# Rotating 96 images by 90 degrees: hand-placed semaphores and loads cut into 32 KB reads

## The chip, the cores and the metric

The kernel runs on one core of a Trainium2 chip. A core has several engines that run side by side; here three matter. VectorE (DVE in the profile) transposes blocks. SyncE (SP) and ScalarE (ACT) only issue transfers: SP issues the loads from DRAM into the core's on-chip memory, ACT issues the stores back to DRAM. The transfers themselves are carried out by 16 DMA engines, which both queues share. The on-chip memory has 128 partitions; a tile is written `[partitions, elements]`.

The metric is the device time of one execution in microseconds (us), the median of several runs.

## The reference

```python
def setup_inputs():
    batch, c, h, w = 32, 3, 256, 256
    return {"x": np.random.randn(batch, c, h, w).astype(np.float32)}

def reference(x):
    return np.rot90(x, k=1, axes=(-2, -1)).astype(np.float32)
```

Each of the 96 images of 256 x 256 float32 values (256 KB) is turned by 90 degrees: `out[i, j] = x[j, 255 - i]`. No arithmetic is done; 25.17 MB are read and 25.17 MB written.

## The kernel before

The 96 images are worked in six groups of G = 16 images (4.19 MB). A group is loaded into a tile S, turned from S into a tile U, and U is stored. There are three buffers for S and three for U. A tile framework sets the semaphores: it makes SP wait before it loads into an S buffer that is still being read, makes VectorE wait for loads and for U buffers still being stored, and makes ACT wait for the transposes. Within an engine, instructions run in program order.

VectorE's `transpose` works on blocks of 32 partitions by 32 elements. Partitions hold neighbouring rows of an image, so a block transposition moves data between the 32 partitions of a group of 32, and the access patterns of source and destination, with `::-1` where the order is reversed, do the rest of the rotation within a partition. No transfer needs to reach elements one by one: each partition is filled from one contiguous run in DRAM and emptied into one.

Two kinds of groups are used (`KINDS = [1, 2, 2, 2, 2, 1]`):

- Kind 1, the first and the last group: the group is cut into four parts of 1 MB. A partition holds R = 8 rows of an image, a run of 8 KB. Four loads (L44) are issued, then for each part one transpose of 128 x 2048 elements (L49) and one store (L50).
- Kind 2, the four groups between: a partition holds R = 16 rows, runs of 16 KB. Two loads of 2 MB each (L60) fill the two halves of S. Then 16 transposes of 128 x 512 elements (L65) read both halves, and two stores of 2 MB each (L67) empty U.

All loads stand in SP's queue and all stores in ACT's. In the trace the loads' DMA queue is q1 and the stores' is q10. The DMA engines see a transfer as packets, one for each contiguous run (8 KB or 16 KB here), plus small ones (under 512 B) that announce completion, 16 for each transfer.

Of the kernel before, what the change touches and what calls it, by code (L numbers as in the profile page):

```python
# [1 line left out]

# [4 lines left out]


@with_exitstack
def kernel(  # L10
    ctx: ExitStack,
    tc: tile.TileContext,
    x: bass.AP,
    out: bass.AP,
):
    nc = tc.nc
    B, C, H, W = x.shape
    assert H == W == 256
    N = B * C
    P = 128  # L20
    G = 16
    KINDS = [1, 2, 2, 2, 2, 1]
    assert len(KINDS) * G == N
    F = G * H * W // P
    fp32 = mybir.dt.float32

    xf = x.rearrange("b c h w -> (b c h w)").rearrange("(g f) -> g f", g=N // G)
    of = out.rearrange("b c h w -> (b c h w)").rearrange("(g f) -> g f", g=N // G)

    in_pool = ctx.enter_context(tc.tile_pool(name="in_pool", bufs=3))  # L30
    out_pool = ctx.enter_context(tc.tile_pool(name="out_pool", bufs=3))

    for g, kind in enumerate(KINDS):
        S = in_pool.tile([P, F], fp32, name="S")
        U = out_pool.tile([P, F], fp32, name="U")
        if kind == 1:

            R = 8
            Sv = S.rearrange("p (s f) -> p s f", s=4)
            Uv = U.rearrange("p (s f) -> p s f", s=4)  # L40
            xv = xf[g].rearrange("(s p f) -> s p f", s=4, p=P)
            ov = of[g].rearrange("(s p f) -> s p f", s=4, p=P)
            for s in range(4):
                nc.sync.dma_start(out=Sv[:, s], in_=xv[s])  # L44
            for s in range(4):

                src = Sv[:, s].rearrange("p (r k q) -> p q r k", r=R, q=R)[:, ::-1, :, ::-1]
                dst = Uv[:, s].rearrange("p (q k r) -> p q r k", q=R, r=R)
                nc.vector.transpose(dst, src)  # L49
                nc.scalar.dma_start(out=ov[s], in_=Uv[:, s])  # L50
        else:


            R = 16
            Sv = S.rearrange("p (b f) -> p b f", b=2)
            Uv = U.rearrange("p (a f) -> p a f", a=2)
            xv = xf[g].rearrange("(b a qk f) -> b qk a f", b=2, a=2, f=F // 2)
            ov = of[g].rearrange("(b a qk f) -> a qk b f", b=2, a=2, f=F // 2)
            for b in range(2):
                nc.sync.dma_start(out=Sv[:, b], in_=xv[b])  # L60

            src = Sv.rearrange("p b (r k q) -> p q r k b", r=R, q=R)[:, ::-1, :, ::-1]
            dst = Uv.rearrange("p a (q k r) -> p q r k a", q=R, r=R)
            for q in range(R):
                nc.vector.transpose(dst[:, q], src[:, q])  # L65
            for a in range(2):
                nc.scalar.dma_start(out=ov[a], in_=Uv[:, a])  # L67


# [1 line left out]
_INS = ['x']  # L71
_OUTS = [((32, 3, 256, 256), 'float32')]


# [23 lines left out]
```

## Time and profile before

| What | Value |
|---|---|
| Median of 3 runs | 123.97 us (123.87 to 124.13) |
| The profiled execution | 124.01 us |
| Its span, first to last instruction | 122.2 us |
| VectorE busy | 91.3 us (75%), 72 transposes |
| DMA moved | 50.34 MB, 412 GB/s over the span |
| First load issued by SP | 0.73 us |
| First transpose starts | 5.67 us |
| First store issued by ACT | 9.67 us |
| Last transpose | from 106.87 us, 3.97 us long |
| Transfers issued | 16 loads and 16 stores |

Times are counted from the start of the span. Busy time of VectorE is the time in which an instruction runs on it; neighbouring transposes overlap a little, so the sum of single durations is somewhat above it. A DMA share of 1.00 means that all 16 DMA engines had packets under way for the whole window (slightly more than 1.00 can show, since packets at a window's edge are counted to it with their bytes). The list of DMA issues gives the time from issue to landing: a median of 21.1 us for a 2 MB load and 19.0 us for a 2 MB store, 16.6 and 16.1 us for those of 1 MB. That is long beside what 2 MB take at 412 GB/s (5.1 us): the transfers queue behind each other.

### The profile page before, as it was taken

How to read it: one execution, taken by the hardware profiler on the slowest of the kernel's cores; microseconds unless marked ns; L12 is line 12 of the kernel's file. 1: busy time of each engine (PE TensorE's matmuls, PEld its weight loads, DVE VectorE, ACT ScalarE, POOL GpSimd, SP SyncE). 2: the span in 40 equal slices, each digit the busy share in tenths (PEclk: the TensorE clock that was granted, in tenths of full speed). 3: DMA queues.
4: the chain of work that ended last, by engine and by line, in shares of the span. 5: the costliest groups of instructions: out<-in, count | busy, mean ns of one | idle time of the engine just before them, and what ended most of it. 6: DMA issues, size and time to landing. Idle time of an engine off the chain costs nothing.

```text
span 122.2 us, 170 instructions
## 1 busy us (share of the span) xinstructions
DVE 91.3 (75%) x72; POOL 0.2 (0%) x4
## 2 busy tenths in 40 slices
DVE  0199999007999999999999990799999999092000
POOL 0000000000000000000000000000000000000000
DMA  3999999999999999999999999999999999999993
GB/s 86 424 421 416 375 432 429 426 410 442 418 440 437 437 434 418 429 434 429 429 429 429 434 429 421 453 410 413 464 413 429 445 416 426 442 429 408 429 429 161
DMA packets 4609, 50.34 MB, mean 412 GB/s; under 512 B 512, under 2 KB 512, under 8 KB 512
## 3 DMA queue, kind: packets, MB, share of 16 engines
q1 hardware_dynamic: 2304, 25.17, 49.3%
q10 hardware_dynamic: 2304, 25.17, 48.3%
q14 instruction: 1, 0.01, 0.0%
HBM read 25.17 MB, written 25.17 MB: 412 GB/s over the span
## 4 chain that ended last, share of the span: by engine, by line
DMA 61%; DVE 27%; issue 1%; SPq 1%
DMA S<-in_x_dram 46%; DVE U L65 24%; DMA out_dram<-U 16%; DVE U L49 3%; SPq L44 1%
## 5 line engine op out<-in xcount | busy, mean ns | idle before, releaser
L65 DVE STREAM_TRANSPOSE U<-S 128x512 f32<-128x512 f32 x64 | 60.5, 1059 | 10.8 <-DMA S<-in_x_dram 7.1
L49 DVE STREAM_TRANSPOSE U<-S 128x2048 f32<-128x2048 f32 x8 | 31.0, 3937 | 8.7 <-DMA S<-in_x_dram 8.7
L82 POOL MEMSET const-bfloat16-1.0<- 128x1 bf16 x1 | 0.1, 101 | 0.0
L82 POOL MEMSET const-uint8-127<- 128x1 uint8 x1 | 0.1, 101 | 0.0
L82 POOL MEMSET const-float32-0.0<- 128x1 f32 x1 | 0.1, 98 | 0.2 <-issue 0.2
L82 POOL MEMSET const-float32-1.0<- 128x1 f32 x1 | 0.1, 98 | 0.0
## 6 DMA issues: line engine op xcount, KB each, us to landing
S<-in_x_dram SPq DMA_DIRECT2D x8, 2048.0 KB, 21.1
out_dram<-U ACTq DMA_DIRECT2D x8, 2048.0 KB, 19.0
S<-in_x_dram SPq DMA_DIRECT2D x8, 1024.0 KB, 16.6
out_dram<-U ACTq DMA_DIRECT2D x8, 1024.0 KB, 16.1
```

The source lines that it names most:

```text
L44: nc.sync.dma_start(out=Sv[:, s], in_=xv[s])
L49: nc.vector.transpose(dst, src)
L65: nc.vector.transpose(dst[:, q], src[:, q])
L82: nc = _bacc.Bacc("TRN2", target_bir_lowering=False, num_devices=1)
```

## The change

The kernel leaves the tile framework's pools and is synchronised by hand. Everything is inside one critical section (`tc.tile_critical()`), with tensors and semaphores of its own.

- A group is now G = 8 images (2.10 MB), so there are NG = 12 groups, all of one kind. There are six buffers S and six buffers U, 16 KB a partition each.
- A group is loaded in M = 2 halves of 1 MB. A partition gets RI = 8 rows, 8 KB, from each half.
- The loads of group 0 are as those of kind 1 before: 128 runs of 8 KB (L72 of the new kernel). All others go through `load`, which writes out the DMA instruction itself, so that its two sides keep their own shapes: the DRAM side is 32 rows of 8192 elements (32 KB each), the on-chip side 128 partitions of 2048 elements (8 KB each). One 32 KB read fills four partitions.
- Eight transposes of 128 x 512 elements turn a group. Those of one group differ in the row r; each reads, for every column offset q and counting back over k, the two halves b, and writes with a step of eight elements.
- A group is stored with one transfer of 2.10 MB in runs of 16 KB.
- Semaphores: `loaded[s]` counts the landing of a buffer's two loads, `turned` the groups transposed, `stored[u]` the landing of a store. SP waits for `turned` before it loads into a buffer again (group 6 on); VectorE waits for `loaded`, and from group 6 on for `stored`; ACT waits for `turned`. SP closes by waiting for all six `stored`.

The order of instructions on each engine that comes out: SP has 24 loads, the first twelve with no wait; VectorE has 96 transposes, of which the first of each group waits; ACT has 12 stores, each with one wait. SP begins with a NoOp and a branch on which SP, ACT and VectorE wait, and ends with the six waits, another NoOp and a branch that all engines follow.

```diff
-    G = 16
-    KINDS = [1, 2, 2, 2, 2, 1]
+    M = 2
+    G = 4 * M
+    RI, RO = 8, 8 * M
+    FI, FO = RI * W, RO * W
+    FOLD = 32
+    NG = N // G
+    NS = NU = 12 // M
...
+    xv = xf.rearrange("(g b d f) -> g b d f", g=NG, b=M, d=FOLD)
+    xp = xf.rearrange("(g b p f) -> g b p f", g=NG, b=M, p=P)
+    ov = of.rearrange("(g b qk f) -> g qk b f", g=NG, b=M, f=FO)
...
+    def load(dst, src):
+        return nc.sync.add_instruction(
+            mybir.InstDMACopy(
+                name=nc.get_next_instruction_name(),
+                engine=mybir.EngineType.SP,
+                ins=[fixed(src)],
+                outs=[fixed(dst)],
+                queue="qSPDynamicHW",
+                mode="Copy",
+            )
+        )
...
+    ctx.enter_context(tc.tile_critical())
+    S = [ctx.enter_context(nc.sbuf_tensor(f"S{i}", [P, M, FI], fp32)) for i in range(NS)]
+    U = [ctx.enter_context(nc.sbuf_tensor(f"U{i}", [P, FO], fp32)) for i in range(NU)]
...
+    for g in range(NG):
+        s, u = g % NS, g % NU
+        if g >= NS:
+            nc.sync.wait_ge(turned, g - NS + 1)
+        for b in range(M):
+            if g == 0:
+                d = nc.sync.dma_start(out=S[s][:, b], in_=xp[g, b])
+            else:
+                d = load(S[s][:, b], xv[g, b])
+            d.then_inc(loaded[s], 16)
+
+        nc.vector.wait_ge(loaded[s], 16 * M * (g // NS + 1))
+        if g >= NU:
+            nc.vector.wait_ge(stored[u], 16 * (g // NU))
+
+        src = S[s][:].rearrange("p b (r k q) -> p r q k b", r=RI, q=RO)[:, :, ::-1, ::-1]
+        dst = U[u][:].rearrange("p (q k r) -> p r q k", q=RO, r=RI)
+        for r in range(RI):
+            t = nc.vector.transpose(dst[:, r], src[:, r])
+        t.then_inc(turned, 1)
+
+        nc.scalar.wait_ge(turned, g + 1)
+        nc.scalar.dma_start(out=ov[g], in_=U[u][:]).then_inc(stored[u], 16)
+
+    for u in range(NU):
+        nc.sync.wait_ge(stored[u], 16 * len(range(u, NG, NU)))
```

The function `fixed` only wraps an access pattern so that it is kept as it is given. The loop bodies of both kinds of groups, the pools and the framework's tiles are removed.

More of the change, by code (lines that the diff above doesn't have):

```diff
@@ L20 @@
     P = 128
-    G = 16
-    KINDS = [1, 2, 2, 2, 2, 1]
-    assert len(KINDS) * G == N
-    F = G * H * W // P
-    fp32 = mybir.dt.float32
[L27 to L67, printed above, removed]
@@ new lines, with fixed @@
+    M = 2
+    G = 4 * M
+    RI, RO = 8, 8 * M
+    KO = H // RO
+    FI, FO = RI * W, RO * W
+    FOLD = 32
+    NG = N // G
+    NS = NU = 12 // M
+    fp32 = mybir.dt.float32
+    xf = x.rearrange("b c h w -> (b c h w)")
+    of = out.rearrange("b c h w -> (b c h w)")
+    xv = xf.rearrange("(g b d f) -> g b d f", g=NG, b=M, d=FOLD)
+    xp = xf.rearrange("(g b p f) -> g b p f", g=NG, b=M, p=P)
+    ov = of.rearrange("(g b qk f) -> g qk b f", g=NG, b=M, f=FO)
+    def fixed(ap):
+        return mybir.PhysicalAccessPattern(
+            ap=ap.ap, offset=ap.offset, dtype=ap.dtype, memref=ap.tensor.name,
+            memsetref=ap.tensor.name + "_set", bass_ap=ap,
+        )
@@ new lines, in load @@
+    def load(dst, src):
[8 more added lines that the diff above has]
+            )
+        )
+    ctx.enter_context(tc.tile_critical())
+    S = [ctx.enter_context(nc.sbuf_tensor(f"S{i}", [P, M, FI], fp32)) for i in range(NS)]
+    U = [ctx.enter_context(nc.sbuf_tensor(f"U{i}", [P, FO], fp32)) for i in range(NU)]
@@ new lines @@
+    loaded = [ctx.enter_context(nc.semaphore(f"loaded{i}")) for i in range(NS)]
+    stored = [ctx.enter_context(nc.semaphore(f"stored{i}")) for i in range(NU)]
+    turned = ctx.enter_context(nc.semaphore("turned"))
+    for g in range(NG):
[18 more added lines that the diff above has]
+        nc.scalar.dma_start(out=ov[g], in_=U[u][:]).then_inc(stored[u], 16)
```

## The prediction

> **What bounds the kernel now.** I read the page first, then the table of windows, then the DMA view of four windows. The page (row 3: packets, MB and the share of 16 engines' span that the packets took; row 5: the two kinds of transpose):
>
> ```profile
> span 122.2 us, 170 instructions
> ...
> DMA packets 4609, 50.34 MB, mean 412 GB/s; under 512 B 512, under 2 KB 512, under 8 KB 512
> ...
> q1 hardware_dynamic: 2304, 25.17, 49.3%
> q10 hardware_dynamic: 2304, 25.17, 48.3%
> ...
> L65 DVE STREAM_TRANSPOSE U<-S 128x512 f32<-128x512 f32 x64 | 60.5, 1059 | 10.8 <-DMA S<-in_x_dram 7.1
> L49 DVE STREAM_TRANSPOSE U<-S 128x2048 f32<-128x2048 f32 x8 | 31.0, 3937 | 8.7 <-DMA S<-in_x_dram 8.7
> ```
>
> The loads (q1) and stores (q10) together fill 97.6% of the span on all 16 engines, 119.3 us of 122.2. VectorE is busy for 91.3 us (60.5 + 31.0, a little overlapped). So the DMA engines bound it, if they never run dry. The windows say that (start:end, length, VectorE busy, POOL busy, PE clock, DMA share, GB/s):
>
> ```profile
> 12.00:15.00 3.00, 3.00 (x2) 0.00 (x0) 1.00 1.01 363
> ...
> 28.00:43.00 15.00, 14.80 (x16) 0.00 (x0) 1.00 1.00 428
> ...
> 58.00:77.00 19.00, 15.47 (x17) 0.00 (x0) 1.00 1.00 429
> 78.00:105.00 27.00, 25.80 (x19) 0.00 (x0) 1.00 1.01 430
> ...
> 120.00:122.20 2.20, 0.00 (x0) 0.00 (x0) 1.00 0.17 71
> ```
>
> The share is 1.00 in every stage, at 428 to 430 GB/s. The dip to 363 at 12 to 15 us, where the first store joins, costs (428 - 363) x 3 us = 0.195 MB, or 0.46 us. VectorE's and SP's waits in the list of waits (SP: 24.0 us at L60 for stores to leave) cost nothing, since the engines are full meanwhile. What is not data is the first 2.5 us or so and the last 1.5.
>
> **How packets share an engine and what one costs.** The DMA view of four windows (both queues of 16 to 22 us, of 58 to 77 us and of 78 to 92 us, then 112 to 120 us, stores alone):
>
> ```profile
> q1 hardware_dynamic: 122, 1.74, 67.8%
> q10 hardware_dynamic: 120, 0.85, 33.6%
> ```
>
> ```profile
> DMA packets 566, 8.16 MB, mean 429 GB/s; under 512 B 60, under 2 KB 60, under 8 KB 60
> ...
> q10 hardware_dynamic: 284, 4.19, 51.5%
> q1 hardware_dynamic: 282, 3.97, 48.8%
> ```
>
> ```profile
> q10 hardware_dynamic: 274, 3.97, 66.1%
> q1 hardware_dynamic: 279, 2.02, 34.4%
> ```
>
> ```profile
> DMA packets 465, 3.42 MB, mean 427 GB/s; under 512 B 48, under 2 KB 48, under 8 KB 48
> ...
> q10 hardware_dynamic: 465, 3.42, 101.0%
> ```
>
> The packet counts of the two queues are equal in each mixed window, whatever the packets' size: 16 KB loads take two thirds from 8 KB stores (16 to 22), equal sizes share evenly (58 to 77), 8 KB loads get one third beside 16 KB stores (78 to 92). Packet time by size: 8 KB, 3.42 MB in 101.0% of 8 us x 16 engines = 129.3 engine-us, 26.45 GB/s, 310 ns each; 16 KB, 8.16 MB in 100.3% of 19 x 16 = 304.9 engine-us, 26.76 GB/s, 612 ns each. So a packet has a fixed part of 2 x 310 - 612, about 7 ns.
>
> **What the Trainium skill says.** "DMA: Bandwidth & Descriptors", section "Queues, rings and completion order", has each engine round-robin between its queues at packet granularity; the equal counts agree. The same page, "Where 436 GB/s comes from", puts the ceiling at 435 GB/s; 428 to 430 here is 98.5% of it, so at most 1.5%, under 2 us, is to be had from any shape of packet. Its section "Why small descriptors are slow" charges a few cycles per packet; the 7 ns agree. Its "Why a DMA increments its semaphore by 16 and not by 1" says that the outer dimensions of both sides set how many engines take part: 32 DRAM rows and 128 partitions both divide by 16. No run here shows yet a transfer whose two sides are cut differently.
>
> **The change, part by part.**
>
> *Packet sizes.* Before, a third of the bytes (the two groups of L44 and L50) go in 8 KB packets, two thirds in 16 KB. Per engine: 16.78 MB / 16 / 26.45 GB/s = 39.6 us, 33.55 / 16 / 26.76 = 78.4, sum 118.0; with some 1.2 us of stretched packets at the start and at the dip, this is the page's 119.3. After, loads are 2.10 MB in 8 KB (group 0: 5.0 us) and 23.07 MB read in 32 KB. A 32 KB packet, by the same line, is 2 x 612 - 7 = 1217 ns, 26.92 GB/s: 53.6 us. Stores are all 16 KB: 25.17 / 16 / 26.76 = 58.8. Sum 117.3, so -0.7 us. If instead each 8 KB write pays the fixed part, the 23.07 MB take 54.5 us: 118.25, +0.25. These are the two bounds; I take -0.7, because the equal counts show whole packets taking turns[...].
>
> *Loads before stores.* With 32 KB against 16 KB, loads should take two thirds. Twelve loads (12.6 MB, 29 us of DMA) issue at the start with no wait. Group 0's 2.10 MB lands near 8 us (before: 1 MB at 5.67, plus 2.4). Its eight transposes then take 7.5 to 8.5 us (16 of L65 run from 28.20 to 42.85, 0.92 us apart; alone they last 1.06), so the first store is issued near 16 us instead of 9.67. The queued loads cover that: at no cost. Until about 17 us loads move 6.2 MB; the other 19 MB at 285 GB/s last until 84 us; stores have moved 9.5 MB by then, and the 15.7 MB left take 37 us alone: full to about 120 us.
>
> *VectorE.* 72 instructions become 96 of 128x512. The source steps are like L65's and the destination step of 8 elements like L49's, whose rate is 3937 / 4 = 984 ns for 512 elements. So between 0.92 and 1.06 us each: 88 to 102 us in all, ending at 96 to 110 us. The last store's turn comes at 120 - 4.9 = 115 us. Cover 5 us or more; it is gone if the spacing passes 1.10 us.
>
> *New waits.* SP's `turned` wait holds only later loads behind it, and ACT's only later stores; each is one semaphore instead of up to four. VectorE's wait on `stored` (group 6 on) holds its later transposes: group 10 needs store 4, which leaves near 86 us, when VectorE is just ready. A stall of one or two us there lies under the 5 us of cover.
>
> *Issues.* 24 loads and 12 stores for 16 and 16: SP spends 0.4 us on a 1 MB issue against 2.4 us of transfer. The 64 more completion packets lie inside the rates above. POOL's work is the same.
>
> *Start and end.* SP now hands over once more before the first load (a NoOp, then a branch that DVE, ACT and SP wait on), and once more after the last `stored` wait. The close of before, two rounds of such exchanges, lasts from 121.5 to 122.2, so one round is 0.35 us. Bounds: 0.1 (one hop at each end) to 0.7 (a round at each); I take 0.35. The dip at the first store stays in the sum at 0.46 us; it could vanish or double, so +-0.46 in the range.
>
> Sum: 122.2 - 0.7 + 0.35 = 121.85. The profiled execution took 124.01, 1.8 us outside its span, and the median shown is 123.97, so -0.35 us on the median: **123.6 us**, 0.3% faster. About 0.2% (0.25 us) is what a measurement of this kernel can tell from no change.
>
> **The rivals.**
>
> *A, the forecast* (0.64): 123.0 to 124.2 by the bounds on the ends and the dip.
>
> *B, writes pay.* The read is 32 KB and takes its turn as such, but each 8 KB write costs its 7 ns: +0.25 + 0.35 on 123.97 = 124.5. For it: 8 KB packets do show the fixed part. Against: the trace has no packet with unlike sides. 0.15.
>
> *C, loads starve, the other side.* If the engine takes turns by the 8 KB written pieces, or the transfer is cut to 8 KB on both sides so that the 32 KB exist only in the source text, loads get one third, as in 78 to 92 us. Then stores leave as soon as they are ready, and nothing is stored up for the end. When the last load lands, all but two stores are out: 25.17 + 20.97 MB at 428 GB/s, from 2.5 us, 110.9 with landing. Then 7.7 us of transposes, 1.4 us until the store moves, 4.9 us of store and 0.65 to land: 125.5 against 120.7 for full engines. +4.8 + 0.25 + 0.35: **129.4**. It decides once the loads' share falls below about one half; at an even share the backlog just covers the last transposes. For it: the trace shows the one third. Against: what starts a turn is likely the read. 0.16.
>
> *D, VectorE bounds.* Past 1.10 us of spacing each 0.05 us costs 96 x 0.05 = 4.8 us: at 1.15 us, 128.5. Against: both neighbouring patterns are under 1.06. 0.05.
>
> **The numbers.** Faster by over 0.2%: A 0.42. Within: A 0.19, B 0.04. Slower: A 0.03, B 0.11, C 0.16, D 0.05. The range takes A from 123.0, all of B, and the milder part of C and D (a share between one third and one half): 123.0 to 127.0. A alone is 123.0 to 124.2.
>
> **What would show it.** Right: the load queue at two thirds of the share from 17 us on, the last load landing near 84 us, stores alone for some 35 us, DMA share 1.00 to 120 us, about 430 GB/s. Packets of 32 KB at 1217 ns show the -0.7; the time of SP's first issue (0.73 before) and from last landing to end show the handovers. Wrong: a load queue at one third with VectorE waiting for loads and a share below 1 after 110 us (C); 428 GB/s or less with the queues in the forecast order (B); VectorE without gaps to 115 us (D). A rate well under 428 in the 32 KB loads, which nothing here excludes, would break all four.

## The result

| | median | runs | span of the profiled execution |
|---|---|---|---|
| before | 124.02 us | 123.87 to 124.13 (4) | 122.2 us |
| after | 124.76 us | 124.69 to 124.87 (4) | 122.9 us |

The ratio is 1.0061, with a 95% interval of 1.0044 to 1.0079: the change costs 0.74 us. The forecast was 123.6 us, 0.35 us faster. The measured time lies inside the stated range of 123.0 to 127.0 only because that range was stretched for the rivals. The forecast's own range, 123.0 to 124.2, does not hold it, and it lies on the other side of no change.

The page of the changed kernel, in the rows shown of before:

```profile
span 122.9 us, 193 instructions
...
DMA packets 3073, 50.34 MB, mean 410 GB/s; under 512 B 576, under 2 KB 576, under 8 KB 576
...
q1 hardware_dynamic: 1344, 25.17, 48.8%
q10 hardware_dynamic: 1728, 25.17, 47.9%
...
L84 DVE STREAM_TRANSPOSE U<-S 128x512 f32<-128x512 f32 x96 | 93.3, 1273 | 8.3 <-DMA S<-in_x_dram 8.3
```

There are a third fewer packets than before (3073 for 4609), so the reads did become 32 KB. The time in the packets is 96.7% of 122.9 us, 118.8 us, where it was 119.3. VectorE waits once, for its first load, and is busy for 93.3 us (the mean of 1273 ns for one is longer than their spacing of 0.97 us, since neighbours overlap). So VectorE does not bound the kernel, and the record of the DMA engines even shows less work. The windows (start:end, length, VectorE busy, POOL busy, PE clock, DMA share, GB/s) say where they lose:

```profile
16.00:19.00 3.00, 3.00 (x5) 0.00 (x0) 1.00 1.15 481
19.00:23.00 4.00, 4.00 (x6) 0.00 (x0) 1.00 0.98 352
...
28.00:44.00 16.00, 16.00 (x17) 0.00 (x0) 1.00 1.01 434
44.00:58.00 14.00, 14.00 (x16) 0.00 (x0) 1.00 1.01 429
...
92.00:110.00 18.00, 9.62 (x10) 0.00 (x0) 1.00 1.01 432
112.00:118.00 6.00, 0.00 (x0) 0.00 (x0) 1.00 1.01 434
```

Outside the dip the share is about 1 to the end, at 429 to 434 GB/s. The dip at the first store is there, later and no smaller. Its depth can't be read from short windows, since a packet at a window's edge is counted whole and 32 KB packets are large: 481 GB/s stand right before 352. The table in the section after the experiments does without that. What else is lost can lie at the two ends. At the start, the chain of waits of the kernel before and then of the changed kernel reads (start, length, what):

```profile
0.67 0.06 issue
0.73 0.37 SPq L44
```

```profile
0.67 0.05 issue
0.71 0.01 SPq L59
0.73 0.06 issue
0.79 0.03 SPq L117
0.82 0.12 issue
0.95 0.38 SPq L72
```

L59 is the line of the critical section, L117 that of the tile framework's context around it, in the launch. SP passes a NoOp and a branch before its first load at 0.95 us, against 0.73 before: 0.22 us. At the end, the lines of the section and of the launch (engine, instruction, count, durations in ns, first and last start in us; `q` is the engine's instruction queue):

```profile
L59 SPq NOP  x2: 13/13/13, 0.7 to 122.2; - x2
L59 SPq EVENT_SEMAPHORE  x2: 17/22/28, 121.9 to 122.1; - x2
L59 SPq COMPARE_BRANCH  x1: 33/33/33, 121.8 to 121.8; - x1
L59 ACTq DRAIN  x1: 8/8/8, 122.0 to 122.0; - x1
...
```

```profile
L117 POOLq EVENT_SEMAPHORE  x4: 17/17/17, 122.3 to 122.8; - x4
...
```

The same events of the kernel before:

```profile
L93 POOLq EVENT_SEMAPHORE  x4: 17/17/17, 121.6 to 122.1; - x4
```

SP has seen its last store by 121.8 us. The section then closes by an exchange of its own (121.8 to 122.2), and only after that comes the closing barrier that the kernel before had too, 0.7 us earlier. The section's exchange is 0.4 us of that; its last store also lands 0.3 us later, at 121.36 us for 121.06. Start and end together make 0.6 us of the 0.7 by which the spans differ.

### The profile page after: what moved, and what is told of

It is laid out like the page before. It is cut to its first block, busy times and chain, and to the rows that moved or that the text cites. A ratio compares the mean times of both kernels' runs of the same rounds, so it can differ in the third digit from the quotient of the medians.

```text
span 122.9 us, 193 instructions
## 1 busy us (share of the span) xinstructions
DVE 93.3 (76%) x96; POOL 0.2 (0%) x4
## 2 busy tenths in 40 slices
DMA packets 3073, 50.34 MB, mean 410 GB/s; under 512 B 576, under 2 KB 576, under 8 KB 576
## 4 chain that ended last, share of the span: by engine, by line
DVE 73%; DMA 6%; issue 3%; SPq 0%
DVE U L84 73%; DMA S<-in_x_dram 6%; SPq L72 0%; SPq L117 0%; SPq L59 0%
## 5 line engine op out<-in xcount | busy, mean ns | idle before, releaser
L84 DVE STREAM_TRANSPOSE U<-S 128x512 f32<-128x512 f32 x96 | 93.3, 1273 | 8.3 <-DMA S<-in_x_dram 8.3
```

Source lines behind the costliest of these rows:

```text
L84: t = nc.vector.transpose(dst[:, r], src[:, r])
```

## The experiments

Each edit is shown against the changed kernel or the experiment named. All of these kernels compute the whole reference. Each was timed beside the kernel before on the same chip; the ratios are to that.

**1. The section taken away.** The instructions go straight to the engines, without the section and without the tile framework's context around it; the closing barrier and clearing are written out. (The kernel before has that context too, and issues its first load at 0.73 us with it.)

```diff
-    ctx.enter_context(tc.tile_critical())
...
     for u in range(NU):
         nc.sync.wait_ge(stored[u], 16 * len(range(u, NG, NU)))
+    nc.all_engine_barrier()
+    nc.clear_and_free_semaphores(loaded + stored + [turned])
+    nc.all_engine_barrier()
```

> The changed kernel without the critical section and without the tile framework around it: the same loads, transposes, stores and waits, with one closing barrier, a clearing of the semaphores and a second barrier, as the kernel before has. Theory (the handovers at both ends are most of the loss): SP's first issue goes from 0.95 us back to about 0.73, and the time from the last landing to the end from about 1.2 us to 0.8; together -0.5 to -0.6 us, so 124.1 to 124.3 us, level with the kernel before (ratio 1.000 to 1.003). Rival (the loss lies in the transfers): the ends do not move by more than 0.1 us and the time stays at 124.6 to 124.8 (ratio 1.005 to 1.007).

Measured: 124.01 us, ratio 0.9998 (0.9990 to 1.0006), 0.75 us less than the changed kernel (0.8 us by the two ratios) and a little more of a gain than expected. The first load is back at the old place, as the timeline shows (start, length, engine and line):

```profile
0.73 0.85 SPq L71 DMA_DIRECT2D S<-in_x_dram  x2
```

The closing barrier's first GpSimd events are early again, and the span is 122.2:

```profile
L91 POOLq EVENT_SEMAPHORE  x2: 17/17/17, 121.5 to 121.6; - x2
```

So the whole loss against the kernel before is the section's handover at the ends. Without it the new transfers are neither faster nor slower than the old ones, within 0.1 us, and the next question is where the expected 0.7 us of packet time went.

**2. Other packet sizes for the loads.** The first sets `FOLD = 64`, so that loads read 16 KB and write two partitions. The second loads every group as group 0, in 8 KB on both sides. The third does that for groups 0 to 5 only.

```diff
-    FOLD = 32
+    FOLD = 64
```

> One number changed: the DRAM side of the loads is 64 rows of 16 KB instead of 32 rows of 32 KB (each read fills two partitions of 8 KB). Theory (the fixed part of a packet is worth only about 3 to 4 ns, since neighbouring packets overlap in the record; and the dip at the first store grows with the size of the load packets in flight): 44 packets more an engine cost +0.15 us, the dip gets 0.1 to 0.3 us smaller; 124.5 to 124.8 us. The queues share evenly. Rival 1 (7 ns a packet, as predicted): +0.3 us with the dip unchanged, 125.0 to 125.1. Rival 2 (32 KB reads are themselves slow): 0.4 us or more faster, 124.3 or less.

```diff
-            if g == 0:
+            if True:
```

> All loads as those of group 0: 128 runs of 8 KB on both sides, no 32 KB reads. Theory (whole packets take turns, whatever their size): loads get one third beside 16 KB stores, the last load lands near 111 us, VectorE waits for loads, the DMA engines run dry while the last group is turned: +4 to +6 us, 129 to 131 us. Rival (the sharing is not by packets, or the backlog lasts anyway): under +1 us, 125.0 to 125.8.

```diff
-            if g == 0:
+            if g < 6:
```

> Groups 0 to 5 (the twelve loads issued without a wait, in flight when the first store starts) in 8 KB runs, groups 6 to 11 in 32 KB reads. Theory (the dip at the first store grows with the load packets' size): the dip at 16 to 24 us shrinks from about 0.7 us to 0.3 or less, against some 0.4 us for more packets (120 an engine at 3.5 ns): 124.5 to 124.9 us. Rival (the dip is a cost of the first store alone): dip as before, more packets: 125.1 to 125.3. In either case loads get one third until the 8 KB loads are through, so the last load lands later than the 87 us or so of the changed kernel, without the engines running dry.

Measured: 126.55 us (ratio 1.0194, 1.0179 to 1.0210), 130.31 us (1.0500, 1.0484 to 1.0516) and 125.32 us (1.0100, 1.0083 to 1.0116). The 16 KB loads cost 1.8 us where neither theory had more than 0.3, so my idea of the sharing was off. The DMA view of 26 to 46 us of the changed kernel shows how (packets, MB, share):

```profile
DMA packets 480, 8.65 MB, mean 433 GB/s; under 512 B 112, under 2 KB 112, under 8 KB 112
...
q1 hardware_dynamic: 240, 5.24, 60.9%
q10 hardware_dynamic: 240, 3.41, 39.8%
```

The queues take equal turns, 240 and 240, but the loads get 61%, not two thirds. The small completion packets (112 of them here) take turns as well. Per engine a 1 MB load is two packets of 32 KB and a completion, three turns for 64 KB, 21.3 KB a turn. A 2 MB store is eight packets of 16 KB and a completion, nine turns for 128 KB, 14.2 KB a turn. That makes 60%. For 16 KB loads the same count gives five turns for 64 KB, 12.8 KB a turn, or 47%: less than half. A turn is one record: linked end to start, the records that start in 28 to 44 us form 16 chains, one for each engine, and in 327 of the 360 steps along them the queue changes. (The section of the Trainium skill that the prediction cites for the turns, "Queues, rings and completion order" in "DMA: Bandwidth & Descriptors", counts some 9 to 17 descriptors to a turn; with one descriptor for each run, the trace does not agree with that number.) In the same window of that kernel:

```profile
q10 hardware_dynamic: 306, 4.49, 52.4%
q1 hardware_dynamic: 302, 4.13, 48.3%
```

So stores catch up, VectorE waits for loads seven times (22.8 us in all, 8.2 of it for the first load), and when the last load has landed nothing is left to do while the last group is turned. The windows of that kernel at the end:

```profile
100.00:110.00 10.00, 7.54 (x8) 0.00 (x0) 1.00 1.00 426
...
114.00:119.00 5.00, 2.92 (x4) 0.00 (x0) 1.00 0.51 216
```

Half of the engines' time in these 5 us is idle, about 2.4 us. With 8 KB loads (nine turns for 64 KB, 33%; measured 35.3% in 26 to 44 us) the hole is deeper:

```profile
116.00:122.00 6.00, 4.60 (x5) 0.00 (x0) 1.00 0.21 87
```

This is the prediction's rival C, brought about by the 8 KB loads: priced at 129.4 us, it came to 130.3, inside the 129 to 131 expected here. It shows what the 32 KB reads are worth in this scheme. They keep the loads' share above one half; the time of the packet itself is the smaller part.

The third kernel does not run dry, yet its dip at the first store is the deepest of all, 257 GB/s in one slice of the page, and the second kernel's is nearly as deep (6.34 MB moved in 12 to 28 us against 6.28; the changed kernel moves 6.55). I had expected it to shrink with the size of the load packets, and it grew. The rival's number, 125.1 to 125.3, was nearly met, but not for its reason, a dip as before.

**3. Warming the store queue.** One small transfer by ACT at the start: a load, then a store whose place is written again later, then the same store in the kernel before.

```diff
+    nc.scalar.dma_start(out=W[:], in_=wv).then_inc(warm, 16)
+    nc.scalar.wait_ge(warm, 16)
```

> The kernel of e1_no_section, with one small load (128 x 128 floats, 64 KB, into a tile that nothing reads) issued by ACT at the very start, before any store. Theory A (the dip at 16 to 24 us is the first use of ACT's DMA queue): it moves to the start, where the engines are idle; GB/s in 16 to 24 us goes from about 390 to 425 or more, and the time falls by 0.4 to 0.8 us to 123.2 to 123.6 us. Theory B (the dip is the first writing to DRAM beside reads): dip as before, time 124.1 to 124.3 (64 KB more).

```diff
+    nc.gpsimd.memset(W[:], 0.0).then_inc(filled, 1)
+    nc.scalar.wait_ge(filled, 1)
+    nc.scalar.dma_start(out=wv, in_=W[:]).then_inc(warm, 16)
+    nc.scalar.wait_ge(warm, 16)
```

> The kernel of e1_no_section, with one small store (128 x 128 floats of zeros, 64 KB) issued by ACT at the start, into a part of the output that the first real store writes again later. Theories A and B (first use of ACT's queue, or first write to DRAM): both are over before the engines are full, so the dip at 16 to 24 us is gone and the time is 123.2 to 123.6 us. Theory C (the dip comes each time that stores join loads after a pause, or from the first 2 MB store itself): dip as before, 124.0 to 124.3 us.

```diff
+    W = w_pool.tile([P, 128], fp32, name="W")
+    nc.gpsimd.memset(W[:], 0.0)
+    nc.scalar.dma_start(out=wv, in_=W[:])
```

> The kernel before, with the same small store by ACT ahead of all others. Theories A and B: its dip at 12 to 15 us (363 GB/s) goes to 420 or more and the time falls by about 0.4 us, to 123.6 us. Theory C: dip and time as before (124.0 to 124.3 us).

Measured: 124.37 us (ratio 1.0028, 1.0019 to 1.0036), 124.37 us (1.0023, 1.0012 to 1.0033) and 124.27 us (1.0020, 1.0013 to 1.0028). In the new scheme the dip stays: 379 and 377 GB/s in 16 to 24 us, 367 without the warming. So there it is neither the first use of ACT's queue nor the first write. Both kernels come out above the times expected of a dip that stays. The small transfer itself has a price: without its own bytes they have moved 0.09 and 0.13 MB less than experiment 1 by 12 us, which is 0.2 to 0.3 us.

In the kernel before, the dip did get smaller (410 GB/s in 12 to 16 us, 379 without), about half of it by the MB moved, so neither theory fits both kernels. The time did not fall, because the gain only pays for the small store: by 12 us this kernel is 0.12 MB behind the kernel before, by 28 us and by 116 us level with it. What is left is one of the 16 engines, which ends at 121.29 us (121.06 before), while the completions of the other 15 are through by 120.75 us in both. Why that one is later I can't say.

**4. What the dip depends on.** Four S buffers instead of six (from experiment 1), so that fewer loads are queued ahead of the first store:

```diff
-    NS = NU = 12 // M
+    NS, NU = 4, 6
```

> The kernel of e1_no_section with four S buffers instead of six: eight loads stand in SP's queue when the first store is issued, not twelve. Theory D (the dip at the first store grows with the loads that are queued ahead of it): GB/s in 16 to 28 us rises from about 385 to 405 or more, 123.6 to 123.8 us. Theory E (the dip comes from the first 2 MB store with its 16 KB runs, whatever is queued): dip as before, 123.9 to 124.2 us, as loads still run ahead of the stores and the backlog still covers the last transposes.

Then the store of group 0 in two parts of 8 KB runs, in four of 4 KB runs, and all stores in two parts of 8 KB runs (all from experiment 1; the counts of `stored` follow):

```diff
+        if g == 0:
+            for h in range(2):
+                c = slice(h * FO // 2, (h + 1) * FO // 2)
+                nc.scalar.dma_start(out=ov[g, :, :, c], in_=U[u][:, c]).then_inc(stored[u], 16)
```

> The kernel of e1_no_section with the store of group 0 cut into two of 1 MB, in 8 KB runs, as the kernel before starts. Theory E (the dip is that of the first store's 16 KB packets): the dip falls from about 0.9 us to the 0.55 of the kernel before, 123.6 to 123.8 us. Theory D: dip as before, 124.0 to 124.2 us.

> The kernel of e9_split_store with the store of group 0 cut into four of 512 KB, in 4 KB runs. Theory (the dip grows with the packets of the first store): a further 0.1 to 0.2 us less dip against 0.1 us for 16 more packets an engine: 123.8 to 124.0 us. Rival (any smaller first store gives the same, or the dip moves to the first 16 KB store): 123.95 to 124.2 us.

> The kernel of e1_no_section with every store cut into two of 1 MB in 8 KB runs. It prices a packet: 96 more data packets and 12 more completion packets an engine. If a packet costs 3 to 5 ns of the engine's time (theory: most of the 7 ns in the record is overlap of neighbours), +0.3 to +0.5 us; if it costs the 7 ns that were predicted, +0.7 us or more. Against it stands the smaller dip at the first store, as in e9_split_store (-0.1 to -0.4 us). Theory: 123.8 to 124.2 us; rival (7 ns): 124.3 to 124.7 us. A load takes 3 turns for 64 KB and an 8 KB store 9 turns for 64 KB, so loads should hold 75% of the engines where both are queued.

Measured: four buffers 124.14 us (ratio 1.0006, 0.9998 to 1.0013); two parts 123.94 us (0.9987, 0.9980 to 0.9994); four parts 123.83 us (0.9989, 0.9981 to 0.9997); all stores in 8 KB 124.26 us (1.0030, 1.0016 to 1.0044).

Four buffers instead of six change nothing that can be told. Over 16 to 28 us the rate did rise from 385 to 407 GB/s, the sign that theory D asked for, but that is packets at the window's edge: in 12 to 28 us the two kernels move 6.53 and 6.50 MB. How the first store is cut does change the dip: windows of 12 to 28 us, first of experiment 1, then with two parts, then with four:

```profile
12.00:28.00 16.00, 16.00 (x18) 0.00 (x0) 1.00 1.00 403
```

```profile
12.00:28.00 16.00, 16.00 (x18) 0.00 (x0) 1.00 1.00 412
```

```profile
12.00:28.00 16.00, 16.00 (x18) 0.00 (x0) 1.00 1.00 422
```

From 403 to 422 GB/s is 0.3 MB or 0.7 us by 28 us. The cut makes the runs shorter and the transfers smaller at once, and which of the two counts is not shown. Not all of the gain is kept, because there is a second, smaller dip once the first 16 KB store follows (6.81 MB in 28 to 44 us with four parts, 6.91 without; 6.88 where all stores are in 8 KB). What is left is 0.1 to 0.2 us. These two are the only versions here that come out ahead of the kernel before, by 0.1%; their intervals overlap with that of experiment 1.

The last kernel prices a packet. The DMA view of 92 to 112 us, stores alone, in 8 KB and then (experiment 1) in 16 KB:

```profile
DMA packets 1170, 8.54 MB, mean 427 GB/s; under 512 B 128, under 2 KB 128, under 8 KB 128
```

```profile
DMA packets 591, 8.63 MB, mean 432 GB/s; under 512 B 64, under 2 KB 64, under 8 KB 64
```

With packets at the edges counted in part these are 8.55 and 8.63 MB: the 8 KB runs move 0.077 MB less, 0.18 us, for 32 data and 4 completion packets more an engine, or 5 ns each. That is the upper end of the "3 to 5" of that expectation; the 7 ns of the prediction are too many. The time fell between the two theories. In the three kernels with cut stores VectorE waits 1.6 to 7.4 us for stores to leave, and the time does not show it: the backlog of stores covers that.

## Why the prediction was wrong, step by step

To set the steps against each other I added up the MB moved up to a time, each packet's bytes spread evenly over its duration in the trace:

```
up to us          12      28     116
before          3.97   10.60   48.42
after           3.94   10.49   48.35
experiment 1    4.05   10.55   48.43
two parts       4.05   10.70   48.50
four parts      4.04   10.82   48.54
8 KB loads first 3.91  10.19   48.03
before, warmed  3.85   10.61   48.42
```

The last two rows are the third kernel of experiment 2 and the third of experiment 3 (without the small store's own bytes). At 430 GB/s, 0.043 MB is 0.1 us, and 16 us move 6.88 MB. Before and experiment 1 issue their first load at the same time and close in the same way, so their difference is the transfers alone. By 12 us experiment 1 is 0.07 MB ahead (0.04 of it by 4 us already, when both still load in 8 KB runs); in 12 to 28 us it loses 0.12 MB; after that it gains 0.06 MB. There is one trace of each kernel, so a few hundredths of a MB can be chance.

The forecast was missed by 1.1 us, and two terms of its sum failed. For the transfers it had -0.7 us, where experiment 1 shows none; for the ends it had +0.35, where the section cost 0.75. The first is the larger miss, and it decides the sign: with 0 for the transfers, even +0.35 for the ends makes the kernel slower, while 0.75 for the ends beside -0.7 for the transfers makes a sum of +0.05, no change.

- *What bounds the kernel*: right. The share of the DMA engines is about 1 from 3 us to 120 us in both kernels; all that counted was packets, the dip and the ends.
- *Packet sizes, -0.7 us*: the step that failed most, right in sign and too large. Shown by bytes moved, the gain is (0.07 + 0.06) / 0.43, about 0.3 us, or less by what the first 4 us hold. Two things made it small. The price of a packet was read from summed packet times, but neighbouring packets overlap a little in the record (shares of 1.01 with 8 KB), so that such a sum counts some time twice; by MB moved it is 5 ns, not 7 (the prediction's own figures, 2 x 310 - 612, make 8). For the 96 packets an engine that were saved (4609 - 3073, over 16), 5 ns make an estimate of 0.5 us. And the line was carried on to 32 KB reads, which no trace then showed. Beside stores they are near the 1217 ns forecast (on average 1213 for those that start in 28 to 44 us, 1227 in 44 to 60, 1221 in 60 to 92), the sign that was to show the -0.7. But in 11 to 18 us, loads alone, the changed kernel's 96 such packets take 1242 ns on average, as long as four 8 KB packets (309 each), at 423 GB/s: there the long reads gain nothing, 0.15 us or so.
- *The dip, taken as unchanged with +-0.46*: it is about 0.3 us deeper than before (0.12 MB), inside the bound that I gave. Before, the first stores were of 1 MB in 8 KB runs; now they are of 2 MB in 16 KB, and the split stores of experiment 4 show that this matters. That took away the rest of the packet gain. That the two cancel to within 0.1 us is chance.
- *Start and end, +0.35 us, bounds 0.1 to 0.7*: the other step that failed. The mechanism was right and the size half of what it should be. Taking the section away gives 0.75 us, a little outside the bounds (the 0.6 of the trace is inside). The trace shows 0.22 us at the start and 0.4 at the end. I had priced both handovers together as one round of the closing barrier. In fact the section's exit alone takes as long as such a round, and its entry two thirds of one.
- *Sum*: +0.75 for the ends, -0.3 for packets, +0.3 for the dip, against +0.74 measured.
- *Loads before stores*: the mechanism is right and its size nearly. Loads hold 61% of the engines rather than two thirds, since completions take turns, and the last of them lands at 90 us rather than 84. The backlog of stores covers the last transposes, as forecast.
- *VectorE*: right. 96 transposes take 93.3 us, 0.97 us apart, ending at 101.6 us (forecast 96 to 110), with no wait for `stored`.
- *Rival B* came nearest in time (124.5), by luck for the most part. That each 8 KB write pays for itself fits the 1242 ns of 11 to 18 us and not the 1213 to 1227 ns beside stores; the rest of the lost time lay in the ends and the dip. *Rival C* did not happen, but experiment 2 shows its mechanism and its price where the read size is smaller.

What stays open: what the dip at the first store is. It begins before the stores' data do: in experiment 1 the first store is issued at 16.05 us and its first data packet starts at 21.07, but the loads are down to 369 GB/s in 19 to 20 us already; before, the first store's packet starts at 13.84 us and the loads move 357 GB/s in 12 to 13. So turns between the recorded packets are not what starts it. Why it depends on how the first store is cut, is deepest beside 8 KB loads and returns in part for the first 16 KB store is open, as is why 32 KB reads are slower in 11 to 18 us than just before.

## What to carry to other kernels

Where the transfer engines are full in every stage, as here, what a rewrite can still change is small, and the fixed parts at the two ends (0.75 us) weigh more than what a third fewer packets saved (0.3 us): read the instructions between the barrier and the first load, and between the last landing and the end, and price each exchange for itself. Where two queues share the engines in equal turns, choose packet sizes so that the queue that feeds the last stage stays ahead (here 61% for the loads was enough, and 48% was not), and count the completion packets as turns. Check the price of a packet against the MB that a stage moved, and not against summed packet times alone.

## What was not expected of the hardware

- Completion packets take a turn like data: a queue with three turns for 64 KB beside one with nine turns for 128 KB gets 61%, and with 8 KB stores (nine turns for 64 KB) 73% against a count of 75%.
- A dip comes at the first store, before its data start. By the table, 12 to 28 us lose from 0.2 us (four parts: 6.78 MB moved) to 1.4 us (8 KB loads first: 6.28 MB) against 6.88 MB. With loads of 32 KB it shrinks as the first store is cut (runs of 16, 8 and 4 KB: 403, 412 and 422 GB/s over 12 to 28 us). Four load buffers instead of six leave it as it is, and a small store done ahead does not take it away in the new scheme.
- A 32 KB read into four partitions is one packet and one turn. Beside stores it takes 1213 to 1227 ns on average, less than four 8 KB packets; in 11 to 18 us, loads alone, 1242 ns, as long as four (309 ns each).
- Entering and leaving one critical section costs 0.6 us in the trace and 0.75 us in the timed runs; experiment 1 computes the reference without either exchange.
